# Gathering a value cache sample by sample, and fetching one attention head earlier, in a hybrid decoder layer on one core

## The chip, the core and the metric

The kernel runs on one core of a Trainium2 chip. The core has a matrix engine (TensorE, "PE" in the profile; its weight loads are a row of their own, "PEld"), a vector engine (VectorE, "DVE"), a scalar engine (ScalarE, "ACT"), GpSimd ("POOL") and SyncE ("SP", which here does nothing but start transfers). Each engine works through its own list of instructions in order; engines wait for one another by semaphores. Transfers between the core's memory (SBUF) and HBM are done by 16 DMA engines that all issuing engines share. The metric is the time of one execution in microseconds (us); smaller is better.

## The reference

The program computes one layer of a hybrid decoder for two groups of requests that share the weights: a prompt of 1024 tokens, and 8 samples of 4 new tokens each, which have 256 tokens in a paged cache. Cut to what matters here:

```python
h = rmsnorm(x, norm_mix_w)
q_a, k_a, v_a, u, z, a, b, g_a, g_b = split(h @ w_in)
# branch A: stick-breaking attention, 8 heads of 64
beta = sigmoid(q.k / 8 + sb_bias);  w = beta * prod(1 - beta of the keys between)
o_a  = w @ v            # prompt: its own keys; samples: pages of cache_k, cache_v, then their new rows
# branch B: short convolution, SiLU, gated delta rule with a 128x128 state, 4 heads
o_b, ssm_new = gdn_branch(short_conv(u), z, a, b, ssm_prev)
x = x + (sigmoid(g_a) * (o_a @ w_pa) + sigmoid(g_b) * (o_b @ w_pb)) @ w_o
x = x + relu(rmsnorm(x) @ w_up)**2 @ w_down
```

The pages of a sample are named by a table of indices (`page_table`), so the rows of `cache_k` and `cache_v` are gathered: two transfers of 256 KB for a sample's keys and two for its values.

## The kernel before, in words

Every matrix product that has to be exact is done as three products of a high and a low part (`dense`, lines 134 to 139): `w_hi x_hi`, `w_hi x_lo`, `w_lo x_hi`. A 128-column block of a weight is loaded by SP into a staging tile (`ws_...`, one buffer), ACT writes its high part (`wh_...`, line 127) and DVE the low part (`wl_...`, line 128). The input rows stay in SBUF as `xh`, `xl`, in four column chunks of 256, 256, 256 and 288.

The program is written as a sequence of stages, and a scheduler orders the instructions of each engine at build time by priority and by where buffers come free. So the work of neighbouring stages is interleaved, in a fixed order. `tc.issue_after(x)` keeps an instruction behind `x`. A tile tag with `bufs=n` has n slots that its tiles share; a tile gets a slot when the last reader of the former tile is done.

Around the change the order of the program is:

1. The prompt's delta rule, four heads (`gdn_head`), with the q, k, v projections of branch A spread among it. The projected q and k go to HBM in a high and a low part (`q_d`, `k_d`), v as rows (`v_d`). These projections use the four slots of the tag `ft` (pool `fk`, `NFT = 4`).
2. The sample stage. `keys(s)` gathers the key pages of sample s into a tile `kg` (two slots), which PE transposes (`dkt`) and ACT evicts into `kts` (four slots). `values(s)` gathers the value pages into a tile `vg` (four slots). Both gathers are started by GpSimd, two transfers for a sample. Before the samples' own delta rule, `keys` and `values` are called for samples 0 to 3. The delta rule is a chain of small steps between PE and DVE: `dmt` and `dMT`, 64 small products `dks` with the state, then three rounds `py`, `dy` (lines 736 to 740), `dpo`, `vexp` (line 763), and the new state. Then comes the samples' attention in two groups g of four samples: scores `dsc` (line 867), weights, `dwt`, values `dav` (line 896). For g = 1 `keys` and `values` of samples 4 to 7 are called inside that loop. The loop ends with `osT`, which is stored to `o_d` (line 906).
3. The gates. 16 jobs, each of one weight block, four chunks of 24 products on PE (`pd_g`), four evictions by ACT (`gt`, line 1042) into one tile of the tag `ft`, and one store of 528 KB (`gA_d`, `gB_d`, line 1044). The first eleven jobs are written ahead of the prompt's attention, and the scheduler spreads them through the sample stage, so that PE always has products to do there. Job names are branch and column block: `gt1_4` is the second gate's block 4.
4. The prompt's attention, 8 heads of 8 row blocks in a pipeline with a lag of four blocks. `stage_a` fetches a head's operands when its first block comes up: `attn_load` starts six transfers of 256 KB into `qs`, `kh`, `kl` (two slots each, in the pool `ak`), and `load_v` one of 512 KB for a pair of heads. `scores` does the products (`sc`, lines 937 and 938, into the PSUM tag `d` of two slots; the gates' chunks use the tag `f`, also two slots), ACT the sigmoid (line 939), GpSimd the mask and 1 - s (lines 940, 943), DVE the running product (line 947). The pool `ak` lies where the sample stage's pool `bk` was, and so its first transfers wait until `bk`'s tiles are done.
5. Filled into that pipeline are the last five gate jobs and nine residual steps: each loads 128 raw rows of x (`xr`, line 1049), transposes 32x32 blocks on DVE (`xs`, line 1052, in the tag `ft`), and stores them to `xT_d` in four transfers of 4096 pieces of 128 bytes (line 1055). `xT_d` is read much later, from line 1252 on.

The tag `zz` (pool `zp`, one slot) holds z of the delta rule, and later `ofb0`, a part of branch B's output.

Of the kernel before, what the change touches and what calls it, by code (L numbers as in the profile page):

```python
# [18 lines left out]
P = 128  # L19
D = 1024  # L20
NP = 1024
NS = 32
T = NP + NS
NSEQ = 8
# [14 lines left out]
def hybrid_step(ctx, tc, x_prompt, x_sample, cache_k, cache_v, page_table, state_conv, state_ssm,  # L39
# [5 lines left out]
    V, S_, G, PE, SY = nc.vector, nc.scalar, nc.gpsimd, nc.tensor, nc.sync  # L45
# [103 lines left out]
    q_d = [dr.tile([4, P, NP], F32, name=f"q{x}_d") for x in "hl"]  # L149
    k_d = [dr.tile([4, P, NP], F32, name=f"k{x}_d") for x in "hl"]  # L150
# [24 lines left out]
    ksT = keep.tile([P, 4, NS], F32, name="ksT")  # L175
    vsT = keep.tile([P, 4, NS], F32, name="vsT")
    m84 = keep.tile([P, 8], F32, name="m84")
# [431 lines left out]
    def values(s):  # L609
        vgs[s] = bk.tile([P, 2, 512], F32, tag="vg", name=f"vg{s}", bufs=4)  # L610
        for pg in range(2):
            G.indirect_dma_start(vgs[s][:, pg, :], None, cvf, bass.IndirectOffsetOnAxis(ap=idx[:, 2 * s + pg:2 * s + pg + 1], axis=0))

    for s in range(4):
        keys(s)
        values(s)
    dctx = ExitStack()
    dk = pool("dk", stack=dctx, side="right")
    blkf = blk.rearrange("p b t -> p (b t)")
# [97 lines left out]
    pmt = gtile("dmt")  # L717
    tr(pmt[:, 0:P], dM)
    dMT = dk.tile([P, P], F32, name="dMT")
    V.tensor_copy(dMT, pmt[:, 0:P])  # L720
    pks = gtile("dks")
    for i, i0 in enumerate((4, 0)):
        kz = dk.tile([P, GH, NSEQ, NS], F32, tag="big", name=f"kz{i}")
# [11 lines left out]
    dy = dr_  # L735
    for it in range(3):
        py = gtile(f"dy{it}")
        PE.matmul(py[:, 0:P], lhsT=dMT, rhs=dy, start=True, stop=True)
        dy = dk.tile([P, P], F32, tag="dyt", name=f"dyt{it}", bufs=2)
        V.tensor_tensor(dy, dr_, py[:, 0:P], op=ALU.subtract)  # L740
    pod = gtile("dpo")
    PE.matmul(pod[:, 0:P], lhsT=dA, rhs=dy, start=True, stop=True)
    don = dk.tile([P, P], F32, name="don")
# [16 lines left out]
    dkp = dk.tile([P, P], F32, name="dkp")  # L760
    V.tensor_scalar(dkp, knd, degc, None, op0=ALU.mult)
    vexp = dk.tile([P, NSEQ, P], F32, tag="big", name="vexp")
    V.tensor_tensor(vexp, dy.unsqueeze(1).to_broadcast([P, NSEQ, P]), m84.unsqueeze(2).to_broadcast([P, NSEQ, P]), op=ALU.mult)
    for h in range(GH):
        V.tensor_tensor(sst[:, :, h, :], sst[:, :, h, :],
                        egb[:, 8 * h:8 * h + 8].unsqueeze(2).to_broadcast([P, NSEQ, P]), op=ALU.mult)
# [82 lines left out]
    for p in range(4):  # L849
        for a in range(2):  # L850
            V.tensor_copy(qbd[64 * a:64 * a + 64, :, p, 2 * p + a, :],
                          qsT[64 * a:64 * a + 64, p, :].rearrange("p (s t) -> p s t", s=8))
    osT = bk.tile([P, 4, NS], F32, name="osT")
    for g in range(2):
        psc = ttile(f"dsc{g}")
        if g:
            for s in range(4, 8):
                keys(s)
        kts = [kts_[4 * g + s4] for s4 in range(4)]
        for s4 in range(4):  # L860
            s = 4 * g + s4
            V.tensor_copy(kts[s4][:, :, 256:260], ksT[:, :, 4 * s:4 * s + 4])
            if g:
                values(s)
        for p in range(4):
            for s4 in range(4):
                PE.matmul(psc[32 * s4:32 * s4 + 32, 0:260], lhsT=qbd[:, 4 * g + s4, p].rearrange("p h t -> p (h t)"),
                          rhs=kts[s4][:, p, :], start=(p == 0), stop=(p == 3))
        n = 260
        ds_ = bk.tile([P, n], F32, tag="ds", name=f"ds{g}")  # L870
        S_.activation(ds_, psc[:, 0:n], AF.Sigmoid, bias=brow, scale=HD ** -0.5)
        V.tensor_tensor(ds_[:, 256:260], ds_[:, 256:260], mnew, op=ALU.mult)
        da = bk.tile([P, n], F32, tag="da", name=f"da{g}")
        V.tensor_scalar(da, ds_, -1.0, 1.0, op0=ALU.mult, op1=ALU.add)
        dp = bk.tile([P, n], F32, tag="dp", name=f"dp{g}")
        V.memset(dp[:, n - 1:n], 1.0)
        V.tensor_tensor_scan(dp[:, n - 2::-1], da[:, n - 1:0:-1], da[:, n - 1:0:-1], 1.0, op0=ALU.mult, op1=ALU.bypass)
        V.tensor_tensor(ds_, ds_, dp, op=ALU.mult)
        wx = bk.tile([P, 8, 4], F32, tag="wx", name=f"wx{g}")
        V.memset(wx, 0.0)  # L880
        V.tensor_tensor(wx[:, 4 * g:4 * g + 4, :], sgrp.unsqueeze(2).to_broadcast([P, 4, 4]),
                        ds_[:, 256:260].unsqueeze(1).to_broadcast([P, 4, 4]), op=ALU.mult)
        pw = ttile(f"dwt{g}")
        for pg in range(2):
            tr(pw[:, pg * P:(pg + 1) * P], ds_[:, pg * P:(pg + 1) * P])
        tr(pw[0:32, 2 * P:3 * P], wx.rearrange("p s t -> p (s t)"))
        dw = bk.tile([P, 2, P], F32, tag="dw", name=f"dw{g}")
        S_.activation(dw.rearrange("p a b -> p (a b)"), pw[:, 0:2 * P], AF.Copy)
        dwn = bk.tile([32, P], F32, tag="dwn", name=f"dwn{g}")
        S_.activation(dwn, pw[0:32, 2 * P:3 * P], AF.Copy)  # L890
        pav = ttile(f"dav{g}")
        for pg in range(3):
            for s4 in range(4):
                rs = slice(32 * s4, 32 * s4 + 32)
                if pg < 2:
                    PE.matmul(pav[rs, :], lhsT=dw[:, pg, rs], rhs=vgs[4 * g + s4][:, pg, :], start=(pg == 0), stop=False)
                else:
                    PE.matmul(pav[rs, :], lhsT=dwn[:, rs], rhs=vsn, start=False, stop=True)
        om = bk.tile([P, 8, HD], F32, tag="om", name=f"om{g}")
        V.tensor_tensor(om, pav.rearrange("p (h d) -> p h d", h=8), m84.unsqueeze(2).to_broadcast([P, 8, HD]), op=ALU.mult)  # L900
        pos = ttile(f"dos{g}")
        for p in range(4):
            PE.matmul(pos[:, p * 16:(p + 1) * 16], lhsT=om[:, 2 * p:2 * p + 2, :].rearrange("p h d -> p (h d)"),
                      rhs=sel.rearrange("p a b -> p (a b)"), start=True, stop=True)
        V.tensor_copy(osT[:, :, 16 * g:16 * g + 16], pos[:, 0:64].rearrange("p (a b) -> p a b", a=4))
# [8 lines left out]
    def attn_load(hh):  # L914
        p, a = hh // 2, hh % 2
        rs = slice(64 * a, 64 * a + 64)
        qs = ak.tile([P, NP], F32R, tag="qs", name=f"qs{hh}")
        kh = ak.tile([P, NP], F32R, tag="kh", name=f"kh{hh}")
        kl = ak.tile([P, NP], F32R, tag="kl", name=f"kl{hh}")

        for r in range(2):
            hs = slice(64 * r, 64 * r + 64)
            SY.dma_start(qs[hs].bitcast(F32), q_d[r][p, rs])
            SY.dma_start(kh[hs].bitcast(F32), k_d[0][p, rs])
            SY.dma_start(kl[hs].bitcast(F32), k_d[1][p, rs])
        return qs, kh, kl

    def scores(blk):
        hh, i = blk
        qs, kh, kl = heads[hh]  # L930
        n = P * (i + 1)
        qsl = slice(i * P, n)
        s = ak.tile([P, NP], F32, tag="s", name=f"s{hh}_{i}", bufs=LAG + 2)
        for k0 in range(0, n, 512):
            kn_ = min(512, n - k0)
            pt = dtile(f"sc{hh}_{i}_{k0}")
            PE.matmul(pt[:, :kn_], lhsT=qs[:, qsl], rhs=kh[:, k0:k0 + kn_], start=True, stop=False)
            last = PE.matmul(pt[:, :kn_], lhsT=qs[:, qsl], rhs=kl[:, k0:k0 + kn_], start=False, stop=True)
            S_.activation(s[:, k0:k0 + kn_], pt[:, :kn_], AF.Sigmoid, bias=sbb[:, hh:hh + 1], scale=HD ** -0.5)
        G.affine_select(s[:, qsl], s[:, qsl], pattern=[[-1, P]], compare_op=ALU.is_gt, fill=0.0, base=0,  # L940
                        channel_multiplier=1)
        am = ak.tile([P, NP], F32, tag="am", name=f"am{hh}_{i}", bufs=2)
        G.tensor_scalar(am[:, :n], s[:, :n], -1.0, 1.0, op0=ALU.mult, op1=ALU.add)  # L943

        pr = ak.tile([P, NP], F32, tag="pr", name=f"pr{hh}_{i}")
        am_r = am[:, n - 1:0:-1]
        V.tensor_tensor_scan(pr[:, n - 1:0:-1], am_r, am_r, 1.0, op0=ALU.mult, op1=ALU.bypass)  # L947
        V.tensor_tensor(s[:, :n - 1], s[:, :n - 1], pr[:, 1:n], op=ALU.mult)
        return s, last
# [9 lines left out]
            S_.activation(wt[:, b0 * P:(b0 + bn) * P], pt[:, :bn * P], AF.Copy)  # L959
        return wt  # L960

    heads, vns, oTs, wts = {}, {}, {}, {}

    def load_v(p):
        vn = ak.tile([P, NC, P], F32, tag="vn", name=f"vn{p}", bufs=2)
        SY.dma_start(vn, v_d[p])
        return vn
# [41 lines left out]
    def stage_a(x):  # L1009
        if x >= NB:  # L1010
            return
        hh, _ = blks[x]
        if hh not in heads:
            if hh // 2 not in vns:
                vns[hh // 2] = load_v(hh // 2)
            heads[hh] = attn_load(hh)
        state[x] = scores(blks[x])

    def stage_b(x, fill):
# [53 lines left out]
    for x, (j, b) in enumerate(gjobs[11:]):  # L1073
        for c in range(len(CX)):
            fills.append(lambda j=j, b=b, c=c: gate_step(j, b, c))
            t = 4 * x + c
            if t % 2 == 0 and t // 2 < 9:
                fills.append(lambda t=t // 2: residual_step(t))
    pipeline(0, SPLIT, fills)
    ofb0 = zp.tile([P, 4, 256], F32, tag="zz", name="ofb0")  # L1080
    SY.dma_start(ofb0, o_d[4:8, :, 0:256].rearrange("k p c -> p k c"))
# [585 lines left out]
```

## Time and profile before

| | us |
|---|---|
| three runs | 1724.34, 1724.98, 1728.57 (median 1724.98) |
| the profiled execution | 1733.34 |
| its span, first to last instruction | 1731.6 |
| PE busy in it | 1682.5 (97%) |
| DVE, ACT, POOL busy | 1153.2, 773.3, 200.4 |
| mean granted PE clock | 0.993 |

PE is the engine that the end hangs on almost everywhere: 88% of the chain that ended last is PE's work. A change can only help where PE stands still or is granted a lower clock. In the listings, a row of the timeline has its start, its duration, the engine, the line, the operation with output and inputs, and in brackets the idle time ahead of it with what ended it. "Issue" means idle time that no semaphore in the profile explains. A row of the windows view gives, for one stretch, the busy time of PE, PEld, DVE, ACT and POOL with the number of instructions, then the granted clock (1.00 is full), the busy share of the DMA engines and GB/s.

### The profile page before, as it was taken

To read this page: it belongs to the slowest core of one execution; us is meant where nothing else is said; L and a number is where in the kernel's file an instruction comes from. 1 tells how busy PE (TensorE), PEld (TensorE's weight loads), DVE (VectorE), ACT (ScalarE), POOL (GpSimd) and SP (SyncE) were. 2 spreads that over 40 slices of the span, in tenths; PEclk is the share of its full clock that TensorE was granted. 3 is DMA by queue.
4 is the path that set the end of the run, shared out by engine and by line. 5 is a ranking of instruction groups with operands and counts; after the bars stand their busy time and mean duration, and the time that the engine had idled before them with its cause. 6 is when DMAs were issued, how large, how long until landed. Compare 5 with 4: busy or idle time off the path is not lost.

```text
span 1731.6 us, 34630 instructions
## 1 busy us (share of the span) xinstructions
PE 1682.5 (97%) x13958; PEld 1624.7 (94%) x13958; DVE 1153.2 (67%) x2309; ACT 773.3 (45%) x1542; POOL 200.4 (12%) x243
## 2 busy tenths in 40 slices
PE   7999999999998999999999999999999999999998
PEld 6999999999998788988989989999999999999998
DVE  6665677867243317778766487887777679788743
ACT  5553434343324214564443456554454564344353
POOL 1120111110005114444400000000000000000000
PEclk9999999999999999999999999999999999999999
DMA  5142233234346478977134645555443766433411
GB/s 179 44 122 69 67 107 92 93 118 133 119 138 211 131 185 200 209 196 193 32 118 125 179 140 145 149 148 160 152 137 113 259 217 218 148 117 95 136 68 66
DMA packets 259036, 239.24 MB, mean 138 GB/s; under 512 B 55890, under 2 KB 217011, under 8 KB 258876
## 3 DMA queue, kind: packets, MB, share of 16 engines
q1 hardware_dynamic: 253926, 226.27, 43.9%
q0 software_dynamic: 3200, 10.52, 1.9%
q8 instruction: 110, 1.80, 0.4%
q10 hardware_dynamic: 1750, 0.23, 0.1%
q14 instruction: 50, 0.41, 0.1%
HBM read 163.21 MB, written 73.77 MB: 137 GB/s over the span
## 4 chain that ended last, share of the span: by engine, by line
PE 88%; DMA 4%; DVE 4%; issue 2%; ACT 1%; SPq 0%; DVEq 0%; POOLq 0%; ACTq 0%
PE pu L139 6%; PE pu L137 6%; PE pu L138 6%; PE pw L139 5%; PE pw L138 5%; PE pw L137 5%; PE pd_g L137 3%; PE pd_g L139 3%; PE pd_g L138 3%; PE wt L111 2%; PE po L985 2%; PE pv L137 1%; PE pv L139 1%; PE pv L138 1%; PE px L138 1%
## 5 line engine op out<-in xcount | busy, mean ns | idle before, releaser
L139 PE MATMUL pu<-Xh,ul 128*128 128x264 f32 x812 | 230.1, 284 | 0.0
L137 PE MATMUL pu<-Xh,uh 128*128 128x264 f32 x812 | 229.8, 283 | 0.0
L138 PE MATMUL pu<-Xl,uh 128*128 128x264 f32 x812 | 229.7, 283 | 0.0
L137 PE MATMUL pw<-hc,w 128*128 128x264 f32 x728 | 204.1, 284 | 2.4 <-ACT w L1479 2.4
L138 PE MATMUL pw<-hc,w 128*128 128x264 f32 x728 | 204.6, 285 | 0.0
L139 PE MATMUL pw<-hc,w 128*128 128x264 f32 x728 | 200.8, 285 | 1.0 <-DVE w L1480 1.0
L137 PEld LDWEIGHTS pu<-Xh,uh 128*128 128x128 f32 x812 | 153.2, 189 | 0.1
L138 PEld LDWEIGHTS pu<-Xl,uh 128*128 128x128 f32 x812 | 152.6, 188 | 0.0
L137 PE MATMUL pd_g<-xh,wh_g 128*128 128x256 f32 (+1 forms) x512 | 150.6, 294 | 1.5 <-issue 1.5
L139 PEld LDWEIGHTS pu<-Xh,ul 128*128 128x128 f32 x812 | 152.0, 188 | 0.0
L138 PE MATMUL pd_g<-xl,wh_g 128*128 128x256 f32 (+1 forms) x512 | 149.4, 292 | 1.8 <-issue 1.8
L139 PE MATMUL pd_g<-xh,wl_g 128*128 128x256 f32 (+1 forms) x512 | 149.6, 292 | 1.1 <-issue 1.1
L137 PEld LDWEIGHTS pw<-hc,w 128*128 128x128 f32 x728 | 136.8, 188 | 2.6 <-ACT w L1479 2.6
L138 PEld LDWEIGHTS pw<-hc,w 128*128 128x128 f32 x728 | 136.2, 188 | 0.0
L139 PEld LDWEIGHTS pw<-hc,w 128*128 128x128 f32 x728 | 134.3, 188 | 1.4 <-DVE w L1480 1.4
L947 DVE TENSOR_TENSOR_SCAN pr<-am 128x127 f32<-128x127 f32 (+7 forms) x64 | 87.9, 1376 | 42.7 <-POOL am L943 42.6
L139 PEld LDWEIGHTS pd_g<-xh,wl_g 128*128 128x128 f32 x512 | 98.0, 191 | 5.9 <-issue 5.7
L137 PEld LDWEIGHTS pd_g<-xh,wh_g 128*128 128x128 f32 x512 | 97.9, 191 | 4.7 <-issue 4.0
L138 PEld LDWEIGHTS pd_g<-xl,wh_g 128*128 128x128 f32 x512 | 97.9, 191 | 2.6 <-issue 2.0
L1479 ACT ACTIVATE w<-a 128x512 fp32r<-128x512 f32 x78 | 43.4, 620 | 88.4 <-PE pw L139 77.0
L139 PE MATMUL px<-mh,wl_wo 128*128 128x264 f32 x256 | 72.4, 285 | 1.3 <-DVE wl_wo L1231 1.2
L138 PE MATMUL px<-ml,wh_wo 128*128 128x264 f32 x256 | 72.6, 285 | 0.0
(577 smaller groups left out, 5071.1 us busy)
## 6 DMA issues: line engine op xcount, KB each, us to landing
hc_d<-t SPq DMA_DIRECT2D x26, 924.0 KB
hc<-hc_d SPq DMA_DIRECT2D x87, 264.0 KB
a<-in_w_down_dram SPq DMA_DIRECT2D x48, 256.0 KB
ws_g<-in_w_in_dram SPq DMA_DIRECT2D x16, 512.0 KB
ws_wo<-in_w_o_dram SPq DMA_DIRECT2D x32, 256.0 KB
ua<-in_w_up_dram SPq DMA_DIRECT2D x16, 512.0 KB
ub<-in_w_up_dram SPq DMA_DIRECT2D x16, 512.0 KB
gA_d<-gt SPq DMA_DIRECT2D x8, 528.0 KB
```

Of the source, the lines that this page charges most:

```text
L111: PE.transpose(out, in_, ident[:k, :k])
L137: PE.matmul(pt[:, :n], lhsT=wh[k], rhs=xh[k], start=(k == 0), stop=False)
L138: PE.matmul(pt[:, :n], lhsT=wh[k], rhs=xl[k], start=False, stop=False)
L139: PE.matmul(pt[:, :n], lhsT=wl[k], rhs=xh[k], start=False, stop=(k == nk - 1))
L947: V.tensor_tensor_scan(pr[:, n - 1:0:-1], am_r, am_r, 1.0, op0=ALU.mult, op1=ALU.bypass)
L985: PE.matmul(po[64 * r:64 * r + 64, 0:P], lhsT=vn[:, b, rs], rhs=wts[hh, 2 * m + r][:, b * P:(b + 1) * P], start=(b == 0), stop=(b == 2 * m ...
L1479: S_.activation(tl[:, 0], src, AF.Copy)
```

## The change

Three things are edited.

First, the value gathers of samples 0 to 3 no longer follow the key gathers. They take their row indices from a second tile `idxv`. A helper `values_at(mark, ss)` copies the two columns of a sample from `idx` to `idxv` on DVE, behind a given DVE instruction (`mark`), and the gathers wait for that copy. The marks are the copy `dMT` for sample 0, the first and the third round `dy` for samples 1 and 2, and `vexp` for sample 3. For samples 4 to 7 the mark is the copy of the new keys into `kts`.

Second, the operands of attention head 0 are no longer fetched by `attn_load` into the pool `ak`. They are fetched ahead of the samples' attention by `fetch_head`, `qs0` into the slot of `zz`, `kh0` and `kl0` into two of the four slots of `ft`. These slots are given back after head 0's last scores. `ofb0`, which also uses `zz`, now waits for that. The values of a pair of heads are loaded as before.

Third, the residual steps come later in the list of fills: the step that stood behind fill 0, 2, 4, ... 16 now stands behind 3, 5, 7, ... 19.

```diff
     def values(s):
         vgs[s] = bk.tile([P, 2, 512], F32, tag="vg", name=f"vg{s}", bufs=4)
         for pg in range(2):
-            G.indirect_dma_start(vgs[s][:, pg, :], None, cvf, bass.IndirectOffsetOnAxis(ap=idx[:, 2 * s + pg:2 * s + pg + 1], axis=0))
+            G.indirect_dma_start(vgs[s][:, pg, :], None, cvf, bass.IndirectOffsetOnAxis(ap=idxv[:, 2 * s + pg:2 * s + pg + 1], axis=0))
 
     for s in range(4):
         keys(s)
-        values(s)
+    idxv = bk.tile([P, 16], I32, name="idxv")
+
+    def values_at(mark, ss):
+        with tc.issue_after(mark.ins):
+            V.tensor_scalar(idxv[:, 2 * ss[0]:2 * ss[-1] + 2], idx[:, 2 * ss[0]:2 * ss[-1] + 2], 0, None, op0=ALU.add)
+        for s in ss:
+            values(s)
...
-    V.tensor_copy(dMT, pmt[:, 0:P])
+    values_at(V.tensor_copy(dMT, pmt[:, 0:P]), [0])
...
-        V.tensor_tensor(dy, dr_, py[:, 0:P], op=ALU.subtract)
+        mark = V.tensor_tensor(dy, dr_, py[:, 0:P], op=ALU.subtract)
+        if it != 1:
+            values_at(mark, [1 + it // 2])
...
+    values_at(mark, [3])
...
+    def fetch_head(p, rs, tiles):
+        for r in range(2):
+            for tl, src in zip(tiles, (q_d[r], k_d[0], k_d[1])):
+                SY.dma_start(tl[64 * r:64 * r + 64].bitcast(F32), src[p, rs])
+        return tiles
+
+    head0 = fetch_head(0, slice(0, 64), [zp.tile([P, NP], F32R, tag="zz", name="qs0")]
+                       + [fk.tile([P, NP], F32R, tag="ft", name=f"{nm}0", bufs=NFT) for nm in ("kh", "kl")])
     for g in range(2):
...
-            V.tensor_copy(kts[s4][:, :, 256:260], ksT[:, :, 4 * s:4 * s + 4])
+            mark = V.tensor_copy(kts[s4][:, :, 256:260], ksT[:, :, 4 * s:4 * s + 4])
             if g:
-                values(s)
+                values_at(mark, [s])
...
-    heads, vns, oTs, wts = {}, {}, {}, {}
+    heads, vns, oTs, wts = {0: head0}, {}, {}, {}
...
-            if t % 2 == 0 and t // 2 < 9:
-                fills.append(lambda t=t // 2: residual_step(t))
+            if t % 2 == 1 and t >= 3:
+                fills.append(lambda t=(t - 3) // 2: residual_step(t))
```

The scheduler's order changes with it. On POOL, the list of gathers from the start of the sample stage (`kg` keys, `vg` values, the digit is the sample; x2 are a sample's two transfers; `drk` and `df` are powers for the delta rule) was before:

```order
L599 DMA kg0_4347<-in_cache_k_dram,idx_4341 128x512 x2
L612 DMA vg0_4363<-in_cache_v_dram,idx_4341 128x512 x2
L599 DMA kg1_4366<-in_cache_k_dram,idx_4341 128x512 x2
L612 DMA vg1_4382<-in_cache_v_dram,idx_4341 128x512 x2
L612 DMA vg2_4401<-in_cache_v_dram,idx_4341 128x512 x2
L612 DMA vg3_4420<-in_cache_v_dram,idx_4341 128x512 x2
L114 TENSOR_TENSOR drk_4500<-drk2_4498,powc_126 128x1
L599 DMA kg2_4385<-in_cache_k_dram,idx_4341 128x512 x2
L599 DMA kg3_4404<-in_cache_k_dram,idx_4341 128x512 x2
```

The same place in the changed kernel:

```order
L599 DMA kg0_4347<-in_cache_k_dram,idx_4341 128x512 x2
L599 DMA kg1_4363<-in_cache_k_dram,idx_4341 128x512 x2
L599 DMA kg2_4379<-in_cache_k_dram,idx_4341 128x512 x2
L114 TENSOR_TENSOR drk_4489<-drk2_4487,powc_126 128x1
L599 DMA kg3_4395<-in_cache_k_dram,idx_4341 128x512 x2
L599 DMA kg4_6339<-in_cache_k_dram,idx_4341 128x512 x2
L612 DMA vg0_4542<-in_cache_v_dram,idxv_4411 128x512 x2
L599 DMA kg5_6355<-in_cache_k_dram,idx_4341 128x512 x2
L599 DMA kg6_6371<-in_cache_k_dram,idx_4341 128x512 x2
L612 DMA vg1_4624<-in_cache_v_dram,idxv_4411 128x512 x2
L612 DMA vg2_4636<-in_cache_v_dram,idxv_4411 128x512 x2
L612 DMA vg3_4662<-in_cache_v_dram,idxv_4411 128x512 x2
```

Eight value gathers have left the head of the list, and each of the later key gathers has to wait for a slot of `kg`. The gathers of `vg4` to `vg7` still follow one another at the end, as before.

On SP, behind the store that ends the sample stage (`o_d<-osT`), the list was before (`vn` values, `qs`, `kh`, `kl` operands, digit = head; `ws_g` a gate's weight):

```order
L906 DMA o_d_130<-osT_6261 128x4x32
L966 DMA vn0_7699<-v_d_139 128x1024
L923 DMA qs0_7701<-qh_d_135 64x1024
L924 DMA kh0_7702<-kh_d_137 64x1024
L925 DMA kl0_7703<-kl_d_138 64x1024
L923 DMA qs0_7701<-ql_d_136 64x1024
L924 DMA kh0_7702<-kh_d_137 64x1024
L1044 DMA gB_d_133<-gt1_4_7475 128x1056
L925 DMA kl0_7703<-kl_d_138 64x1024
L1049 DMA xr0_7853<-in_x_prompt_dram 128x1024
L923 DMA qs1_7918<-qh_d_135 64x1024
```

Five more transfers of head 1 follow there, and then `ws_g0_6`. In the changed kernel it is:

```order
L926 DMA o_d_130<-osT_6266 128x4x32
L977 DMA vn0_7717<-v_d_139 128x1024
L868 DMA qs1_7945<-qh_d_135 64x1024
L868 DMA kh1_7946<-kh_d_137 64x1024
L868 DMA kl1_7947<-kl_d_138 64x1024
L868 DMA qs1_7945<-ql_d_136 64x1024
L1055 DMA gB_d_133<-gt1_4_7493 128x1056
L868 DMA kh1_7946<-kh_d_137 64x1024
L868 DMA kl1_7947<-kl_d_138 64x1024
L1060 DMA xr0_8024<-in_x_prompt_dram 128x1024
L123 DMA ws_g0_6_8093<-in_w_in_dram 128x8x128
L868 DMA qs2_8328<-qh_d_135 64x1024
```

Six transfers fewer stand ahead of `ws_g0_6`; head 2 and `vn1` now follow right behind it, ahead of `ws_g1_6`.

Head 0's keys stand on SP behind the last projected keys, in the changed kernel (`qs0` is some thirty rows earlier):

```order
L821 DMA out_2_dram<-ntk3_6080 128x8x128
L829 DMA kl_d_138<-kf3_5963 128x1024
L868 DMA kh0_6268<-kh_d_137 64x1024
L868 DMA kl0_6269<-kl_d_138 64x1024
L868 DMA kh0_6268<-kh_d_137 64x1024
L868 DMA kl0_6269<-kl_d_138 64x1024
L123 DMA ws_g0_1_6710<-in_w_in_dram 128x8x128
L821 DMA out_3_dram<-ntv3_6209 128x8x128
```

They are four transfers between the last key store and the weight of the third gate job, where nothing stood before.

More of the change, by code (lines that the diff above doesn't have):

```diff
@@ L762, in hybrid_step @@
     vexp = dk.tile([P, NSEQ, P], F32, tag="big", name="vexp")
-    V.tensor_tensor(vexp, dy.unsqueeze(1).to_broadcast([P, NSEQ, P]), m84.unsqueeze(2).to_broadcast([P, NSEQ, P]), op=ALU.mult)
+    mark = V.tensor_tensor(vexp, dy.unsqueeze(1).to_broadcast([P, NSEQ, P]), m84.unsqueeze(2).to_broadcast([P, NSEQ, P]), op=ALU.mult)
+    values_at(mark, [3])
     for h in range(GH):
@@ L916, in attn_load @@
         rs = slice(64 * a, 64 * a + 64)
[L917 to L926, printed above, removed]
+        return fetch_head(p, rs, [ak.tile([P, NP], F32R, tag=nm, name=f"{nm}{hh}") for nm in ("qs", "kh", "kl")])
     def scores(blk):
@@ L1013, in stage_a @@
         if hh not in heads:
-            if hh // 2 not in vns:
-                vns[hh // 2] = load_v(hh // 2)
             heads[hh] = attn_load(hh)
+        if hh // 2 not in vns:
+            vns[hh // 2] = load_v(hh // 2)
         state[x] = scores(blks[x])
```

## The prediction

> **What bounds the kernel now.** I read the page's busy times first, then PE's waits, then the stretches in which PE stands still.
>
> ```profile
> PE 1682.5 (97%) x13958; PEld 1624.7 (94%) x13958; DVE 1153.2 (67%) x2309; ACT 773.3 (45%) x1542; POOL 200.4 (12%) x243
> ...
> q8 instruction: 110, 1.80, 0.4%
> ```
>
> PE is the bound. The change removes no product from it, so it can only give back time in which PE waits or runs at a lower clock: 1731.6 - 1682.5 = 49 us of idle in the span, and what slow clocks add. PE's waits over the span, with total, number and longest:
>
> ```profile
> PE xtp L111 <- DVE sst__148 L198: 10.3, 2, 10.1
> PE sc L937 <- ACT s L939: 4.2, 1, 4.2
> PE pb L138 <- DVE obl L1126: 2.8, 2, 2.3
> PE pcd L684 <- issue: 2.4, 1, 2.4
> PE pd_g L138 <- issue: 1.8, 2, 1.0
> PE pd_g L137 <- issue: 1.5, 3, 0.7
> PE pd_g L139 <- issue: 1.1, 2, 0.7
> PE dks L728 <- issue: 0.6, 2, 0.3
> ```
>
> `xtp` is the start of the program and `pb` a stage that the change doesn't touch. Left are the wait of `sc` and those by "issue", 2.4 + 1.8 + 1.5 + 1.1 + 0.6 = 7.4 us. The timeline of PE shows where most of these lie:
>
> ```profile
> 531.41 0.49 PE L684 MATMUL pcd<-ublk,dgb 128*128 128x128 f32 x2 [2.39 <-issue]
> 533.63 0.37 PE L137 MATMUL pd_g<-xh,wh_g 128*128 128x256 f32 x1 [0.70 <-issue]
> 545.27 0.44 PE L728 MATMUL dks<-sst,kz 128*32 128x128 f32 x6 [0.29 <-issue]
> 611.18 0.29 PE L138 MATMUL pd_g<-xl,wh_g 128*128 128x288 f32 x1 [0.75 <-issue]
> ```
>
> All of them fall into stretches in which GpSimd starts gathers. From its timeline, the first value gather, the last of the first run, a pair of key gathers, and the first and last of the run of eight for samples 4 to 7:
>
> ```profile
> 522.03 0.95 POOL L612 DMA_INDIRECT vg<-in_cache_v_dram,idx  x1 [0.30 <-DMA sst<-in_state_ssm_dram]
> 533.68 0.95 POOL L612 DMA_INDIRECT vg<-in_cache_v_dram,idx  x1 [0.30 <-issue]
> 543.25 0.95 POOL L599 DMA_INDIRECT kg<-in_cache_k_dram,idx  x1 [4.12 <-PE dmt L111]
> 601.26 0.95 POOL L612 DMA_INDIRECT vg<-in_cache_v_dram,idx  x1 [5.39 <-PE dav L896]
> 610.08 0.96 POOL L612 DMA_INDIRECT vg<-in_cache_v_dram,idx  x1 [0.30 <-DMA vg<-in_cache_v_dram,idx]
> ```
>
> The wait of `sc` has its cause in the chain of waits, which there leaves PE:
>
> ```profile
> 631.75 7.35 DMA kl<-kl_d
> 639.17 12.14 DMA ws_g<-in_w_in_dram
> ```
>
> and on ACT and PE:
>
> ```profile
> 638.67 0.38 ACT L1042 ACTIVATE gt<-pd_g 128x256 f32<-128x256 f32 x1 [2.47 <-PE pd_g L139]
> 641.86 0.41 ACT L1042 ACTIVATE gt<-pd_g 128x288 f32<-128x288 f32 x1 [2.81 <-PE pd_g L139]
> 651.39 1.06 ACT L127 ACTIVATE wh_g<-ws_g 128x1024 fp32r<-128x1024 f32 x1 [8.42 <-DMA ws_g<-in_w_in_dram]
> 652.97 0.79 PE L937 MATMUL sc<-kh,qs 128*128 128x512 f32 x1 [4.17 <-ACT s L939]
> ```
>
> A gate's weight needed 12.14 us because it stood behind the operands of heads 0 and 1. ACT works in order: waiting 8.42 us for that weight, it could not evict the score tiles behind it, and PE ran out of PSUM. What the two stalls cost in all, clock included, I take from the windows (520 to 528 and 626 to 640 are the undisturbed neighbours):
>
> ```profile
> 520.00:528.00 8.00, 8.00 (x69) 8.00 (x69) 3.03 (x3) 5.42 (x7) 6.18 (x7) 1.00 1.06 348
> 528.00:540.00 12.00, 7.37 (x38) 6.24 (x37) 1.94 (x11) 3.96 (x9) 7.66 (x9) 0.72 0.75 230
> 626.00:640.00 14.00, 14.00 (x116) 14.00 (x115) 1.34 (x2) 2.89 (x6) 0.00 (x0) 1.00 0.94 242
> 640.00:656.00 16.00, 11.82 (x83) 11.33 (x81) 5.27 (x8) 4.45 (x9) 4.01 (x8) 0.89 1.02 224
> ```
>
> First stall: 69 products take 8.00 us, 0.116 each, so the 38 of 528 to 540 are worth 4.4 us and **7.6 us** are lost. Second: 14.00 / 116 = 0.121, times 83 is 10.0, and **6.0 us** are lost. Together 13.6 us, all that the change can reach directly.
>
> **The value gathers.** Eight gathers leave the head of POOL's list, where twelve ran with 0.3 us between them, and come back as pairs behind `dMT`, `dy` and `vexp`. The bytes stay the same. What a pair beside other work costs PE is shown at 543 to 546: 0.29 twice, 0.6 us. The pairs of keys that are left in the stretch (samples 1 to 3, now earlier) would at that price cost 1.8 us; the four pairs of values fall on 540 to 570, where only that one pair made PE wait. Bounds: nothing is won, if the key gathers and the state's load alone bring the idle time, and 7.6. I take 7.6 - 2.0 = 5.6, nearer the upper end, because the idle time came after eight gathers and more in a row, at 529 (531.41 - 2.39) and at 611, and hardly behind pairs. The run of eight for samples 4 to 7 stays, and with it waits like that at 611.18.
>
> What this adds: eight copies of two columns on DVE. The nearest row, and the last of the marks:
>
> ```profile
> 516.08 0.17 DVE L589 TENSOR_SCALAR idx<-idx 128x16 int32<-128x16 int32 x1
> 565.84 1.22 DVE L763 TENSOR_TENSOR vexp<-dyt,m 128x1024 f32<-128x1024 f32 x1
> ```
>
> and for what waits behind the gathers, from PE's timeline, the transposes of sample 3's keys and the first use of values:
>
> ```profile
> 551.39 0.66 PE L111 MATMUL dkt<-ident,kg 128*128 128x128 f32 x4
> ...
> 599.09 1.92 PE L896 MATMUL dav<-vg,dw 128*32 128x512 f32 x16
> ```
>
> The copies are 8 x 0.17 = 1.4 us on an engine that is busy a third of the time there; PE's gate products cover it, and without that cover it would be 1.4 us in a chain. Behind the copies wait the gathers and, on POOL, the key gathers queued after them. The values of the first group are first read at 599; their last gather now starts after `vexp` at 565.8, some 30 us earlier. The key tiles are tighter. PE's list now has the transposes of samples 1 to 3 some tens of products earlier, and sample 3's gathers end on POOL only shortly before. From the start of its pair at 543.25 to its transposes at 551.39 sample 3 had 8.1 us; by the products that now stand between, at 0.12 us each, I estimate 5. I charge 0.6 us, bounds 0 and 3.
>
> **Head 0 fetched early, raw rows late.** SP's issues at the start and at the end of the stretch:
>
> ```profile
> 626.15 0.36 SPq L906 DMA_DIRECT2D o_d<-osT  x1
> 639.17 0.39 SPq L123 DMA_DIRECT2D ws_g<-in_w_in_dram  x1
> ```
>
> From 626.15 until `ws_g` landed at 651.3 are 25.2 us, for 512 KB of values, 2 x 1.5 MB of heads, 528 KB of a gate, 512 KB of rows and the weight: 5.1 MB, 0.20 MB per us. Without head 0 it is 3.6 MB, 17.8 us, and the weight lands at 643.9 on the old clock. ACT reaches it after the third chunk's eviction (638.67 in the old order, 640 with the scores now ahead of it), waits 4 us, and evicts the fourth chunk at 645. PE meanwhile has scores and one more chunk to do, till 646, since each PSUM tag has a second slot. So PE waits 0 to 1 us and 6.0 - 1.0 = 5.0 us are won (bounds 0 and 6.0).
>
> The six transfers go where there is room: 1 MB of keys after 437 (434.38 + 2.58), with SP idle till the next weight at 450.84 and the DMA engines busy a tenth of the time:
>
> ```profile
> 434.38 2.58 SPq L819 DMA_DIRECT2D kl_d<-kf  x1
> 450.84 0.37 SPq L123 DMA_DIRECT2D ws_g<-in_w_in_dram  x1
> ```
>
> ```profile
> 440.00:450.00 10.00, 9.84 (x91) 9.18 (x86) 3.21 (x9) 3.15 (x7) 0.00 (x0) 1.00 0.10 39
> ```
>
> The stores of two gate jobs:
>
> ```profile
> 466.86 0.33 SPq L1044 DMA_DIRECT2D gA_d<-gt  x1
> 480.86 0.32 SPq L1044 DMA_DIRECT2D gB_d<-gt  x1
> ```
>
> They take 5 us at 0.20 MB per us; uncovered, the weight would be 5 us late, but PE needs it only behind the second job, whose store is at 480.86. `kh0` and `kl0` hold two of the four `ft` slots until head 0's scores end. A gate tile then has to be stored before the job after next evicts into it. Jobs are 14.0 us apart (466.86 to 480.86), so the store has some 16 us; 528 KB at 0.20 is 2.6 us. I charge nothing. The residual steps move by three chunks of some 3 us (638.67 to 641.86), and `xT_d` is read two stages later. I charge nothing there either.
>
> **Sum.** Against the profiled execution: 1733.34 - 5.6 - 5.0 + 0.6 = 1723.3. That execution is 8.4 us above the median of the runs, and the time without a releaser in it is 7.4: some of the first stall may be there only under the profiler. I take three quarters of 5.6, 4.2. Against the median: 1724.98 - 4.2 - 5.0 + 0.6 = 1716.4.
>
> [...]
>
> **Rivals.**
>
> 1. The idle time by "issue" doesn't come from the crowd of gathers but from something that each of them does, or from the state's 2 MB. For it: at 543 two gathers were enough to make PE wait. Against: 0.6 us is the whole of such waits under `dks`, and the other pairs caused none. Only the second term is left: 1724.98 - 5.0 + 0.6 = 1720.6. [...]
> 2. The late weight is only another one. Head 2 and `vn1` now stand ahead of `ws_g1_6`: 3.6 + 1.5 + 0.5 + 0.5 + 0.5 = 6.6 MB, 33 us after 626, at 659 on the old clock, just when ACT reaches it. Where it is late by more than the two PSUM slots cover, the 5.0 are lost again: 1724.98 - 4.2 + 0.6 = 1721.4.
> 3. The change does nothing that counts: without a profiler the first stall is small, and the second moves: about 1725.
> 4. Slower: two `ft` slots are too few. The stores of `gt1_4` and `gt0_5` now stand in the same crowd as heads 1 and 2. The trace has a 512 KB transfer there that took 12.14 us. It decides from a store of over 16 us on: ACT then can't evict, and PE stops. Two stores 6 us late, with 1.8 us of slow clock each (6.0 - 4.2 in the second stall), cost 15.6, against 8.6 won: 1732.
>
> **How the numbers follow.** Chances: forecast 0.55, then 0.15, 0.12, 0.08 and 0.10. The time is the forecast's, 1716.4. Its own range is 1724.98 - 13.6 = 1711 to 1720; with rivals 1 to 3 it reaches 1726, and a little below 1711 for smaller waits that go too, so 1710 to 1726 leaves out rival 4 and the rest of the lower end. A measurement of this kernel tells 0.3%, 5.2 us, from no change, that is 1719.8. Faster: nearly all of the forecast and half of rival 1, 0.61. Slower: 0.09. The same: 0.30.
>
> **What would show it.** Right: no "issue" wait above 0.7 us before 545; granted clock 1.00 between 528 and 540; `sc` no longer waiting for ACT's `s`; `ws_g0_6` landing within 18 us of `o_d<-osT`. The forecast is wrong where PE's "issue" waits still sum to 6 us or more, if `wh_g` waits 8 us or more for a weight between 615 and 670, if PE waits for `dkt`'s gathers, or if `pd_g` waits for `gt`.

## The result and the profile after

The changed kernel takes **1713.39 us** (median of 5 runs, 1713.05 to 1717.45), the kernel before 1726.84 in the same comparison (1724.34 to 1730.54). The ratio is 0.9929 with a 95% interval of 0.9917 to 0.9942: 10 to 14 us faster. Forecast were 1716.4, 8.6 less than before, with a range of 1710 to 1726. So the direction was right and the forecast gain somewhat too small; the experiments below show that of the two causes one was right and one was not, and that a third was missed.

The busy times of the profiled execution (1713.05 us, span 1711.3):

```profile
PE 1676.0 (98%) x13958; PEld 1620.3 (95%) x13958; DVE 1155.2 (68%) x2317; ACT 774.3 (45%) x1542; POOL 207.3 (12%) x243
```

PE does the same 13958 products. Idle in the span are 1711.3 - 1676.0 = 35 us instead of 49, and PE's busy time itself is 6.5 us shorter, for the most part because fewer products ran at a low clock: the mean granted clock is 0.997 instead of 0.993, and 0.004 of 1676 us are 6.7. PE's waits over the span, largest first, with total, number and longest:

```profile
PE xtp L111 <- DVE sst__148 L198: 10.1, 1, 10.1
PE pw L137 <- ACT w L1490: 2.4, 1, 2.4
PE pd_uk L137 <- ACT xh L210: 2.1, 1, 2.1
...
PE sc L948 <- DMA kh<-kh_d: 0.8, 1, 0.8
...
PE pb L138 <- DVE obl L1137: 0.2, 1, 0.2
```

There is no "issue" row any more, no row of `sc` behind ACT's `s` above 0.2, and `pb <- obl`, 2.8 before, is 0.2. The stretches of the two stalls, and the one in which GpSimd now starts eight gathers one behind the other for samples 4 to 7 (columns as before: PE, PEld, DVE, ACT, POOL, granted clock, DMA share, GB/s):

```profile
528.00:540.00 12.00, 12.00 (x109) 11.83 (x112) 5.24 (x23) 9.96 (x20) 4.45 (x5) 1.00 0.66 200
600.00:612.00 12.00, 12.00 (x119) 10.57 (x121) 3.21 (x7) 2.70 (x6) 5.16 (x6) 1.00 0.70 229
640.00:656.00 16.00, 16.00 (x122) 14.31 (x121) 11.55 (x8) 8.42 (x19) 7.86 (x9) 1.00 0.80 211
```

PE stands still in none of them and has its full clock. And the weight, from the timelines of SP and ACT:

```profile
618.75 0.36 SPq L926 DMA_DIRECT2D o_d<-osT  x1
...
625.77 0.43 SPq L123 DMA_DIRECT2D ws_g<-in_w_in_dram  x1
```

```profile
631.39 0.39 ACT L1053 ACTIVATE gt<-pd_g 128x256 f32<-128x256 f32 x1 [2.46 <-PE pd_g L139]
636.76 1.06 ACT L127 ACTIVATE wh_g<-ws_g 128x1024 fp32r<-128x1024 f32 x1 [4.99 <-DMA ws_g<-in_w_in_dram]
637.73 0.39 ACT L1053 ACTIVATE gt<-pd_g 128x288 f32<-128x288 f32 x1
```

`ws_g0_6` landed at 636.7, 18.0 us after the store `o_d<-osT`; the estimate was 17.8. ACT still waits 4.99 us for it, but PE has work for that long: its only wait for `kh`, 0.8 us, comes at 796, far behind this stall.

### The profile page after: what moved, and what is told of

It reads as the page before. It is cut to its first block, busy times and chain, and to the rows that moved or that the text cites. A ratio compares the mean times of both kernels' runs of the same rounds, so it can differ in the third digit from the quotient of the medians.

```text
span 1711.3 us, 34643 instructions
## 1 busy us (share of the span) xinstructions
PE 1676.0 (98%) x13958; PEld 1620.3 (95%) x13958; DVE 1155.2 (68%) x2317; ACT 774.3 (45%) x1542; POOL 207.3 (12%) x243
## 4 chain that ended last, share of the span: by engine, by line
PE 88%; DVE 4%; DMA 4%; issue 2%; ACT 2%; SPq 0%; POOL 0%; DVEq 0%; POOLq 0%; ACTq 0%
PE pu L139 6%; PE pu L137 6%; PE pu L138 6%; PE pw L139 5%; PE pw L138 5%; PE pw L137 5%; PE pd_g L137 4%; PE pd_g L138 4%; PE pd_g L139 4%; PE wt L111 2%; PE po L996 2%; PE px L138 1%; PE px L137 1%; PE px L139 1%; PE pv L139 1%
```

## The experiments

Ratios are to the kernel before, run on the same chip. Below, "lost" is PE's idle time plus (1 - granted clock) times its busy time, summed over windows of 4 us, in the one profiled execution of each kernel. It is given for three places: the first stall (520 to 568), the second (628 to 660) and a third, in which `pb` waits (756 to 796). A fourth column is a slow clock between 568 and 600 that no wait stands ahead of.

| kernel | median us | ratio [95%] | first | second | third | 568–600 |
|---|---|---|---|---|---|---|
| before, first profile | 1724.98 | | 7.8 | 5.4 | 4.1 | 1.7 |
| before, once more | 1725.94 | 1.0003 [0.9991, 1.0014] | 6.9 | 6.8 | 4.2 | 0 |
| gathers alone | 1718.01 | 0.9952 [0.9938, 0.9966] | 1.4 | 4.6 | 1.7 | 6.8 |
| head alone | 1715.83 | 0.9946 [0.9929, 0.9963] | 3.5 | 0.1 | 1.1 | 0 |
| head and rows | 1714.79 | 0.9943 [0.9923, 0.9962] | 3.8 | 0.1 | 0.9 | 0 |
| third stall alone | 1724.15 | 0.9992 [0.9982, 1.0001] | 5.9 | 6.4 | 1.6 | 0 |
| keys of samples 0, 1 first | 1722.36 | 0.9981 [0.9970, 0.9992] | 7.3 | 6.4 | 1.8 | 0 |
| the same with head and rows | 1716.70 | 0.9945 [0.9928, 0.9961] | 3.2 | 0.8 | 0.9 | 5.1 |
| gathers alone, values together | 1718.05 | 0.9955 [0.9941, 0.9969] | 3.0 | 2.3 | 1.6 | 0 |
| changed kernel | 1713.39 | 0.9929 [0.9917, 0.9942] | 0 | 0 | 1.5 | 1.7 |
| changed, once more | 1713.58 | 0.9938 [0.9920, 0.9956] | 0 | 0 | 3.0 | 0 |
| changed, values together | 1715.91 | 0.9939 [0.9924, 0.9955] | 0 | 0 | 0.9 | 6.8 |
| changed, bytes put back | 1720.09 | 0.9967 [0.9951, 0.9982] | 0 | 8.5 | 1.0 | 0 |

### The kernel before, once more

Nothing is edited.

> The kernel before, unchanged, profiled and timed once more. In the first profile PE lost 7.6 us at 528 to 540 and waited three times 0.7 us at 609 to 613, all by "issue", beside the gathers. If these waits belong to the order of the gathers, the second profile shows them again: PE's waits by "issue" sum to 6 to 9 us, and the wait of sc for ACT (4.2 us) is there too. If they differ from execution to execution, they sum to something else, or lie elsewhere. Time against the kernel before: ratio 1.000, within 0.002.

The time repeats within 0.1%. The second and third stall repeat; the first takes another form. PE's waits between 500 and 600:

```profile
PE dkt L111 <- DMA kg<-in_cache_k_dram,idx: 3.9, 1, 3.9
```

No time at all is left without a releaser. From PE's timeline, and POOL's ahead of it:

```profile
529.78 0.82 PE L111 MATMUL dkt<-ident,kg 128*128 128x128 f32 x6
...
544.39 0.33 PE L111 MATMUL dkt<-ident,kg 128*128 128x128 f32 x1
548.67 0.90 PE L111 MATMUL dkt<-ident,kg 128*128 128x128 f32 x3 [3.94 <-DMA kg<-in_cache_k_dram,idx]
```

```profile
535.64 0.95 POOL L612 DMA_INDIRECT vg<-in_cache_v_dram,idx  x1 [0.30 <-issue]
536.61 0.59 POOL L114 TENSOR_TENSOR drk<-drk,powc 128x1 f32<-128x1 f32 x1
537.38 1.00 POOL L599 DMA_INDIRECT kg<-in_cache_k_dram,idx  x1 [0.18 <-PE dmt L111]
538.69 0.95 POOL L599 DMA_INDIRECT kg<-in_cache_k_dram,idx  x1 [0.30 <-issue]
539.95 1.39 POOL L599 DMA_INDIRECT kg<-in_cache_k_dram,idx  x1 [0.30 <-issue]
541.64 1.86 POOL L599 DMA_INDIRECT kg<-in_cache_k_dram,idx  x1 [0.30 <-issue]
```

The four key gathers are those of samples 2 and 3. They start at 537.38, right behind the last value gather (six run in a row there, two more stand ahead of sample 1's keys), although sample 2's slot came free when sample 0's transposes ended near 530.6. Sample 3's second gather is started at 541.64, and the transposes that need it go on at 548.67. So a second reading of the first stall stands beside the forecast's: not the crowd holds PE up, but the keys that are queued behind it. The idle time by "issue" of the first profile, 7.4 us, is 0.0 in this profile and in every one since.

### The halves

The gathers alone (the edits to `values`, `values_at` and its marks), head 0 alone, and head 0 with the late rows:

```diff
-        values(s)
+    idxv = bk.tile([P, 16], I32, name="idxv")
...
+    values_at(V.tensor_copy(dMT, pmt[:, 0:P]), [0])
```

> Only the value gathers are moved; head 0 and the raw rows stay as before. Theory of the prediction: the first stall goes (4 to 7.6 us), the late weight of 639 to 651 stays with its 6 us: 1726.8 - 4 to - 7.6, about 1721, ratio 0.997. In the profile no wait by "issue" around the samples' delta rule, but sc waiting some 4 us for ACT. Rival (the idle time is no matter of the crowd of gathers): ratio 1.000, and "issue" waits of 6 us or more remain.

```diff
+    head0 = fetch_head(0, slice(0, 64), [zp.tile([P, NP], F32R, tag="zz", name="qs0")]
+                       + [fk.tile([P, NP], F32R, tag="ft", name=f"{nm}0", bufs=NFT) for nm in ("kh", "kl")])
...
+    heads, vns, oTs, wts = {0: head0}, {}, {}, {}
```

> Head 0 is fetched early; gathers and raw rows stay as before. Only one row of x stood ahead of the late weight (512 KB of 4.6 MB), so by the prediction's bytes the rows are worth 512 KB / 0.20 MB per us = 2.5 us of the weight's landing, half of it covered: within 2 us of the kernel with head and rows. Rival: the rows' 128-byte stores are what fills the DMA engines, then this kernel is no faster than before (ratio 0.999 to 1.001).

```diff
-            if t % 2 == 0 and t // 2 < 9:
+            if t % 2 == 1 and t >= 3:
```

> Head 0 is fetched early and the raw rows come late; the value gathers stay as before. Theory of the prediction: the late weight goes (5 to 6 us), the first stall stays: about 1721, ratio 0.997, and "issue" waits of 6 us or more in the profile. If the two halves add, the time that this kernel and the one with the gathers alone save sums to the 13.4 us of the whole change; if it sums to less, one half hides behind the other or they need each other.

The gathers alone win 0.0048 x 1725 = 8.3 us, head 0 alone 9.3, the rows on top of it nothing that can be told (0.9943 against 0.9946). About 1721 was expected of the gathers alone and of head and rows; measured are 1718.0 and 1714.8, so both expectations missed. The halves make 17.6 together, but the whole wins only 10.7 to 12.2 by its two ratios. So on top of head and rows the gathers are worth 0.9 to 2.4 us (0.9943 against 0.9938 and 0.9929), which lies inside the intervals; that they take PE's last 3.8 us out of the first stall is seen in the profiles alone. The table shows where they overlap: each half removes most of the third stall, each takes something off the first (head alone leaves 3.5 of 6.9), and the gathers alone shorten the second.

How head alone can touch the first stall is seen in PE's waits from 500 to 800:

```profile
PE dkt L111 <- DMA kg<-in_cache_k_dram,idx: 3.5, 2, 2.3
```

and in the windows 520 to 560 of the kernel before (once more) and of head alone:

```profile
520.00:560.00 40.00, 36.02 (x366) 33.42 (x366) 17.18 (x41) 17.18 (x30) 24.00 (x23) 0.91 0.73 227
```

```profile
520.00:560.00 40.00, 36.47 (x397) 35.13 (x396) 18.43 (x46) 17.62 (x32) 23.09 (x23) 1.00 0.79 233
```

The idle time is nearly the same, 4.0 and 3.5 us. But it is one wait of 3.9 us with a clock of 0.91 over the stretch in the one, and two waits of 2.3 and 1.2 at full clock in the other, 366 against 397 products. What is gone is the slow clock behind the wait.

### The third stall

In VectorE's list of the kernel before, the low part of the last chunk of `ofb` (`obl`) stood behind the long scans of two blocks. Its timeline in the repeated run of before:

```profile
780.08 1.17 DVE L948 TENSOR_TENSOR s<-s,pr 128x895 f32<-128x895 f32 x1
781.17 2.68 DVE L947 TENSOR_TENSOR_SCAN pr<-am 128x1023 f32<-128x1023 f32 x2
783.78 1.53 DVE L1126 TENSOR_TENSOR obl<-ofb,obh 128x1152 fp32r<-128x1152 f32 x1
```

Both halves of the change, by moving the rest of the program, give another order there. One edge puts it right in the kernel before; beside it only a `tb` row next to it and a pair of rows on POOL change places:

```diff
-            V.tensor_tensor(obl[c], st, obh[c].bitcast(F32), op=ALU.subtract)
+            lows[c] = V.tensor_tensor(obl[c], st, obh[c].bitcast(F32), op=ALU.subtract)
...
+        behind = tc.issue_after(lows[3].ins) if blk == (4, 7) else nullcontext()
+        with behind:
             V.tensor_tensor_scan(pr[:, n - 1:0:-1], am_r, am_r, 1.0, op0=ALU.mult, op1=ALU.bypass)
```

> The kernel before with one edge in VectorE's order: the scan of block 7 of head 4 stands behind the low part of the last chunk of ofb (obl), as it does in the kernel with the gathers alone. Theory: the two halves together win less than the sum of the halves (8.3 and 9.3 us apart, 12 to 13 together) because both also remove the same third stall, pb waiting 2.3 us for obl at 787 to 789 with slow products behind it. Then this edit alone wins 2.8 + about 2 of slow clock, 4 to 5 us: 1720.5 to 1721.5 against 1725.3, pb's wait for obl under 0.5 us. Rival: the third stall is worth its idle time only or comes back at the next block: 0 to 2 us, and the halves overlap for another reason.

Now `obl` runs at 779.58, ahead of the scans, and PE's waits between 640 and 900 begin with:

```profile
PE sc L937 <- ACT s L939: 4.1, 1, 4.1
PE pb L137 <- DVE tb L1147: 1.1, 1, 1.1
PE pa L137 <- DVE ga L1196: 0.9, 1, 0.9
PE pb L138 <- DVE obl L1129: 0.5, 1, 0.5
```

2.8 us of waiting for `obl` became 0.5, and 1.1 for `tb` came in its place. Measured are 1.4 us (0.0008 x 1726; the interval reaches from 3.1 to nothing), where 4 to 5 were expected: the rival, that most of it comes back, is nearer. So the third stall is only a part of the overlap.

### Which is it, the keys or the crowd?

First the key gathers of samples 0 and 1 were put ahead of all values:

```diff
     for s in range(4):
         keys(s)
+    for s in range(4):
         values(s)
```

> The kernel before with the loop over samples 0 to 3 split in two: the key gathers of samples 0 and 1 stand ahead of all value gathers on GpSimd, and eight value gathers still run one behind the other. Theory A (PE's loss at 528 to 540 is the wait of the transposes dkt for sample 1's keys, which stood behind two value gathers): that wait of 3.9 us goes or falls under 1.5, and the time falls by 3 to 5 us, 1720 to 1722, or by some 8 us where VectorE's order in the attention stage removes the third stall too (pb waiting for obl). Theory B (the prediction's: the crowd of gathers itself): the crowd is only one pair shorter ahead of sample 1's keys and as long behind; PE loses 5 us or more between 520 and 550 as before, and the time stays within 2 us of 1725 apart from the third stall.

> The kernel before with head 0 early and the rows late, and the key gathers of samples 0 and 1 ahead of all value gathers, instead of the value gathers spread along the delta rule. Theory A (only the keys' place counts): the remaining 3.8 us of dkt's waits for kg go or halve, 1711 to 1713.5, level with the changed kernel, with no copies on VectorE. Theory B (the crowd counts): no better than head and rows without it, 1714 to 1716, with PE's waits between 520 and 550 at 3 us or more.

Only 3.3 us are won, of which the table has 2.4 in the third stall, and PE's wait is still there:

```profile
PE dkt L111 <- DMA kg<-in_cache_k_dram,idx: 4.1, 1, 4.1
```

It looks like the crowd. But `kg` has two slots: the keys of samples 2 and 3 were not moved ahead by this edit, and stand behind all eight values as before. The wait is that of sample 3's keys, and the expectation had named the wrong sample. With head and rows the same edit wins nothing over head and rows alone (0.9945, 0.9943). An edit that does tell the two apart keeps a crowd and moves it as a whole: all eight value gathers of samples 0 to 3 behind one mark, after the keys of all four samples.

```diff
-    values_at(V.tensor_copy(dMT, pmt[:, 0:P]), [0])
+    values_at(V.tensor_copy(dMT, pmt[:, 0:P]), [0, 1, 2, 3])
...
-        if it != 1:
-            values_at(mark, [1 + it // 2])
...
-    values_at(mark, [3])
```

> The kernel with the gathers alone, but all eight value gathers of samples 0 to 3 follow one mark (the copy to dMT), so that they run one behind the other in one crowd, as before, and behind the key gathers of samples 0 to 3. Theory A (what counts is that the keys of samples 2 and 3 no longer stand behind eight value gathers): PE waits 2 us or less for dkt's keys of samples 0 to 3, and the time is that of the gathers alone, 1717 to 1720 against 1725.5; what can wait now are the keys of samples 4 to 7, which stand behind the crowd. Theory B (the crowd is what costs, wherever it stands): PE loses 5 us or more in the 15 us around the crowd, and 1722 to 1725.5 is measured.

> The changed kernel with all eight value gathers of samples 0 to 3 behind one mark (dMT) instead of one sample at a time along the chain. Theory A (keys' place): 1712.5 to 1715, level with the changed kernel; no wait of PE over 2 us between 520 and 570. Theory B (crowd): 5 us or more lost, 1717 to 1720.

POOL's timeline in the first of the two, from the last key gather to the end of the crowd:

```profile
534.01 0.95 POOL L599 DMA_INDIRECT kg<-in_cache_k_dram,idx  x1 [0.30 <-issue]
535.26 0.95 POOL L612 DMA_INDIRECT vg<-in_cache_v_dram,idxv  x1 [0.30 <-DVE kts L877]
...
545.45 0.95 POOL L612 DMA_INDIRECT vg<-in_cache_v_dram,idxv  x1 [0.30 <-issue]
546.71 0.95 POOL L599 DMA_INDIRECT kg<-in_cache_k_dram,idx  x1 [0.30 <-issue]
```

Eight value gathers stand one behind the other with 0.3 us between; before, six did so. The time is that of the spread gathers, 0.9955 against 0.9952. In the whole change the ratio is 0.9939, against 0.9929 and 0.9938 with the gathers spread. Its median of 1715.91 lies between the ranges of the two theories, so that the time alone doesn't decide; but PE loses nothing between 520 and 568 with either. The stretch in the changed kernel with the values together, whose crowd runs from 541.10 to 553.81:

```profile
520.00:560.00 40.00, 40.00 (x422) 38.53 (x422) 18.38 (x45) 18.68 (x34) 25.01 (x23) 1.00 0.77 222
```

So the crowd by itself costs nothing: here two pairs of keys follow right behind it, and PE doesn't yet need them. In the kernel with the gathers alone and the values together, PE still waits for keys in the stretch:

```profile
PE dkt L111 <- DMA kg<-in_cache_k_dram,idx: 3.0, 2, 1.9
```

The larger wait, 1.9, is for the keys of sample 4, which now are the ones behind the crowd; 1.1 is for those of sample 3. Not separated is whether the later start of a key gather costs PE the time, or the bytes of the values that are still under way ahead of it. The transposes also move in PE's list along with the keys.

### The bytes ahead of the weight

In the changed kernel, 1.5 MB are put back where head 0's loads had been: its tiles are stored to a spare tensor.

```diff
-    SY.dma_start(o_d[0:4, :, NP:T].rearrange("h p c -> p h c"), osT)
+    stored = SY.dma_start(o_d[0:4, :, NP:T].rearrange("h p c -> p h c"), osT)
+    with tc.issue_after(stored.ins):
+        for r in range(2):
+            for x, tl in enumerate(head0):
+                SY.dma_start(spare[3 * r + x], tl[64 * r:64 * r + 64].bitcast(F32))
```

> The changed kernel with six stores of 256 KB, head 0's tiles out to a spare tensor, directly behind the store of osT on SyncE, where the kernel before had head 0's loads; every engine's order is otherwise that of the changed kernel. Theory (the second stall was the weight behind 1.5 MB too many in the queue): ACT again waits 5 us or more for ws_g between 630 and 660, PE's sc waits 2 to 5 us for ACT's s, and 4 to 6 us are lost: 1717.5 to 1719.5. Rival (head 0's early scores, not the bytes, removed the stall): PE doesn't wait for s, and the time stays at 1713 to 1714.5.

The second stall is back. ACT's row for the weight, PE's only wait between 500 and 720, and the stretch:

```profile
643.65 1.06 ACT L127 ACTIVATE wh_g<-ws_g 128x1024 fp32r<-128x1024 f32 x1 [10.76 <-DMA ws_g<-in_w_in_dram]
```

```profile
PE sc L953 <- ACT s L955: 6.8, 1, 6.8
```

```profile
632.00:656.00 24.00, 17.25 (x117) 15.13 (x116) 8.50 (x7) 7.89 (x18) 7.01 (x8) 0.86 0.92 205
```

ACT waits 10.76 us for the weight, `sc` 6.8 for ACT, and the time rises by 0.0029 to 0.0038 of 1726, 5.0 to 6.6 us, a little more than was expected. The first transposes of head 0's weights come no later than in the changed kernel (631.7 and 635.0), so it is the bytes in the queue that make the stall. One remark of the expectation holds only roughly: the lists are the changed kernel's elsewhere, but near the place some hundred gate products and ten evictions of ACT changed places with those of the scores, since the scheduler reckons with the stores too.

### The changed kernel, once more

> The changed kernel once more, beside the two others on the same chip. Expected by all theories: 1712 to 1715, a ratio of 0.992 to 0.994 to before; PE without a wait over 1 us between 520 and 720. Where a slow clock near 575, without a wait ahead of it, comes back in this execution, it is a matter of the single execution and not of the gathers' order, since profiles of both orders show it.

1713.58, ratio 0.9938, no wait of PE between 500 and 720. Its six runs reach from 1706.5 to 1718.8, and in the profiled one the prompt's delta rule ends at 500 instead of 505: some 5 us of the scatter arise before the change acts.

## Why the prediction was right or wrong

**The second stall: right, in place, cause and size.** The step "without head 0 it is 3.6 MB, 17.8 us" gave a landing that came true within 0.2 us. ACT was to wait 4 us and waited 4.99; PE was to wait 0 to 1 us and waits for nothing between 500 and 720. 5.0 us were taken; putting the bytes back costs 5.0 to 6.6. Rival 2, the next weight late in its turn, did not come about: PE has no wait there. Rival 4, a lack of `ft` slots, neither: no product of the gates waits for `gt` in the changed kernel. Rival 3, no gain, is excluded by the measured interval.

**The first stall: the cause wrong, the size near by luck.** The step that failed is "because the idle time came after eight gathers and more in a row", which made the crowd on POOL the cause. It was read from idle time without a releaser in one execution. That time has not come back in twelve further profiles, while the loss has: 6.9 us with the keys of sample 3 as the releaser. Moved as a whole, the crowd costs nothing (40.00 us of products in 40.00). What costs is that the keys of samples 2 and 3 were started behind eight value gathers. That 4.2 us came near was luck: by the profiles head 0 alone takes off about half of the 6.9, for which the forecast had charged nothing, and by the times the gathers add only 0.9 to 2.4 to head and rows. The counter-evidence was announced in the prediction itself: "the run of eight for samples 4 to 7 stays, and with it waits like that at 611.18". It stays, and 600 to 612 shows 12.00 us of products in 12.00. Rival 1 said that the gathers would win nothing, 1720.6 in all; alone they win 8.3, and the whole came to 1713.39. The gathers' gain does not hang on the idle time by "issue", which is 0.0 us in all profiles but the first. Whether the idle time by "issue" of the first profile had the same origin as the wait for keys stays open, since it did not come again. The transfers of the instruction queue that this profile shows near it lie at 523 to 524 and 544 to 545, and so none of them ends the waits between 529 and 537.

**The keys: the sign was wrong.** The prediction charged 0.6 us because the keys of sample 3 were to be tighter, 5 us instead of 8.1. The 5 us came true: in the changed kernel the pair is started at 536.21 and its transposes run at 541.01. But freed of the values ahead of them, the keys land in that time, and no `dkt` waits for `kg`, where the repeated run of before waits 3.9. There the same pair needed 8.7 us (539.95 to 548.67), so the 8.1 of the first profile were hardly slack. The worry wasn't empty: with the gathers alone PE waits 1.4 us for just these keys.

**The third stall: missed.** The step was to call `pb` "a stage that the change doesn't touch". The code is untouched, but the scheduler's list is not: `obl` changed places with a scan, and 2.8 us of waiting became 0.2. By itself it is worth 1.4 us, with an interval that reaches nothing; it may be a part of the difference between 1716.4 and 1713.4.

**The three quarters.** The first stall's 5.6 us were cut to 4.2, because the first profile was slow and its idle time might have been the profiler's. Before loses 6.9 there in the second profile, whose 1725.87 us are at the median. By that profile the cut was the wrong way, by some 3 us; the times don't tell, because the halves overlap.

**What doesn't add up.** By the profiles the three stalls should win some 16 us (6.9 + 6.8 + 4.2 - 1.5); the two profiled executions, before once more and the changed kernel, lie 12.8 apart, and timed are 10.7 to 12.2. Two losses outside the stalls are in the way in the changed kernel's execution: 1.7 us by the slow clock between 568 and 600, and 3.6 us more than before ahead of 500 us (20.9 against 17.3), more than half of it in the first 24 us, which no edit touches. Neither is there in the changed kernel's other profile, of 1706.54. The slow clock takes 2.3 us on average in the nine profiles with the gathers or head 0 changed, 0.4 in the four others. With one execution each this is a hint, and no run was made that controls it; the rest is open.

**What was charged at nothing.** Head 0's transfers early: PE is busy 16.82 of 17 us between 437 and 454, and what is lost from 500 to 930 outside the table's columns is 1.0 to 2.0 us in every kernel but the first profile, with head 0 early or not. The late rows: 0.9943 with them, 0.9946 without. The copies of the list on VectorE: no wait of PE names them. All as forecast.

## What to carry to other kernels

A wait without a releaser, seen in one execution, is not yet a cause: profile the unchanged kernel again before pricing it, and read what stands *behind* a crowd in its engine's list, not the crowd. On an engine that starts transfers in order, put first what is needed first; a prefetch whose first reader is 60 us away, like the values here, belongs behind the transfers whose readers come sooner: behind the values the keys of sample 3 made PE wait 3.9 us (before, once more), ahead of them not at all (the changed kernel). And where a scheduler makes the lists, a change moves waits in stages that it doesn't touch (2.8 us for `obl` became 0.2 here), so halves measured alone need not add up to the whole.

## What the runs showed of the hardware

**A long wait of PE cost more than its own length.** In the stretch of the table, behind waits of 3.7 to 6.8 us the windows show 1.3 to 2.9 us more, lost to a low clock; behind single waits of 1.9 to 2.5 us it is nothing in five cases and 1.3 to 1.5 in three, and once it is 1.5 behind three short waits that sum to 0.9 (the changed kernel once more, at 757). So two waits of 2.3 and 1.2 us (head alone) lost 3.5 us where one of 3.9 (before) lost 6.9. A low clock also came without a wait. Between 570 and 586 the changed kernel with the values together has PE busy throughout, with few products:

```profile
568.00:570.00 2.00, 2.00 (x7) 0.73 (x6) 0.70 (x2) 0.00 (x0) 0.00 (x0) 1.00 0.00 0
570.00:572.00 2.00, 2.00 (x7) 0.71 (x5) 0.93 (x2) 0.39 (x1) 0.00 (x0) 0.87 0.21 33
572.00:574.00 2.00, 2.00 (x6) 1.29 (x6) 0.69 (x1) 0.00 (x0) 0.00 (x0) 0.50 0.00 0
...
586.00:588.00 2.00, 2.00 (x27) 1.36 (x30) 1.24 (x2) 0.00 (x0) 0.00 (x0) 1.00 0.78 266
```

The clock is 0.50 for some 14 us, 6.8 us lost. What lowers it was not shown. The length of a wait does not tell it: 2.5 us of waiting lost nothing to the clock (head and rows), waits that sum to 0.9 lost 1.5, and here there is none. Among the products that run there are those of the new state, marked 32*128 in the timeline, where those of the gates are marked 128*128:

```profile
569.45 1.12 PE L778 MATMUL dst<-vexp,dkp 32*128 32x512 f32 x2
571.07 1.71 PE L778 MATMUL dst<-vexp,dkp 32*128 32x512 f32 x2
```

That these products have a part in the low clock is a guess; no run shows it. The slow stretch is in five of the thirteen profiles, of kernels with and without the change, with 1.7 to 6.8 us lost. The three profiled executions that lost 5.1 to 6.8 there lie 2.0 to 6.6 us above the medians of their kernels.

**Gathers.** In the repeated run of before, a key gather of 256 KB that was started at the end of the run of gathers needed some 7 us until its transposes could go on (541.64 to 548.67), and the value gathers ahead started some 1.25 us one after the other (534.39 and 535.64). At that pace, 8 x 1.25, I estimate 10 us of delay by eight gathers for whatever is queued behind them.
